# First keys of the attention as whole rows with turns behind them, retention's gated groups last, backward states beside the chunks

## The chip, the cores and the metric

One NeuronCore of a Trainium2 chip runs the whole program. The metric is the device time of one execution in microseconds; the median of the runs counts. TensorE is called PE below, its weight loads PEld, VectorE DVE, ScalarE ACT, GpSimd POOL, and SyncE, whose queue issues most DMAs, SP.

## The reference

Two layers of a hybrid block run over 1024 latent tokens (a grid of 16 rows by 64 columns) and 256 context tokens, with a model width of 1024, all in fp32.

```python
h = rms_norm(x, norm_w) * (1.0 + scale) + shift
(na_q, na_k, na_v, gla_q, gla_k, gla_v, gla_g, ret_q, ret_k, ret_v, z, g) = split_cols(h @ w_in)
na_l, na_c = na_branch(...)     # window of 8 x 16 neighbours and all context tokens, softmax
gla_l, gla_c = gla_branch(...)  # chunk scan in both directions, gated decay
ret_l, ret_c = ret_branch(...)  # chunk scan in both directions, fixed decay, rotated q and k
# merge_branches, i over (na, gla, ret):
y = y + sigmoid(gs[i]) * ((outs[i] * silu(zs[i])) @ w_branch[i])
x = x + gate * (y @ w_out)
```

A scan carries a state per head from chunk to chunk, forward and backward, and the context tokens come first in both directions. The second layer computes no context outputs. Queries and keys of retention are rotated for the latent tokens only.

## The kernel before, in words

Every large product is one of three products of a split into a high and a low float32r part (`mms`). One stream of such products, called the GEMM stream here, runs through the whole program: `projections` computes column groups of `w_in` in the order retention, GLA, attention v, attention q/k, the 12 g groups, the six z groups in the order of `Z_ORDER`, and `merge` goes on with `w_branch` and `w_out`. `fm` runs a group feature by feature in blocks of 512, 512 and 256 tokens (layer 1: 512 and 512), `tm` token by token.

The order of all instructions is made by `Drv.slot`, called a turn here. In a turn every worker (`drv.spawn`) and the GEMM stream advance twice, each GEMM advance by 3072 x `drv.mult` columns; then evacuations, and the lane (`attention_lane`) advances once; then the weight loader may issue a load (`load_raw`) or a conversion (`conv`: one ACT cast, two POOL subtractions). A `yield` in a lane costs a turn, in a worker half a turn. Where the GEMM stream only yields, PE gets the workers' matmuls alone.

The lane runs `retention`, `gla` and `na` one after the other, each as soon as its projections are done. The two scans have a first phase for all chunks of 128 tokens (c = 8 and 9 are context), which puts chunk states into `S` and passes on the forward ones; then a loop over c = 8 to 1 with `state_step` passes on the backward states, 4 DVE instructions for each c, two c's for each turn; then the second phase computes outputs, one worker for each chunk from 0 up: in `retention` rotation on DVE (`rope`), transposes on PE (`ret_t`), scores and outputs; in `gla` seven levels of decay on POOL, ACT and DVE, with products `gla_lv` on PE. `post` norms an output, transposes it (`post_t`) and stores it.

`na` works on four pairs of heads p, each with 8 window units and, in layer 0, 2 context units. `load_k(p)` loads the keys: two tiles `ks`, each with 64 rows of `nkh` twice, one above the other, and a tile `kl` of low parts. `pair` loads queries and bias, and three turns later issues the scores (`na_sw`, `na_sc`), then softmax, transposes (`na_ptw`, `na_ptc`) and the outputs (`na_o`). A new pair starts every three turns, and the next p's keys are loaded between them, one DMA a turn.

In `z_evac` the gate z is multiplied with a branch's output: groups 0 and 1 belong to the attention, 2 and 3 to GLA, 4 and 5 to retention. z0 and z1 wait until the attention's outputs are stored. For 0 to 3 the result goes to DRAM; for retention it becomes the high and low operand tiles `br`, with which `merge` begins.

Of the kernel before, what the change touches and what calls it, by code (L numbers as in the profile page):

```python
# [36 lines left out]
BR_ORDER = (2, 1, 0)  # L37
Z_ORDER = (2, 3, 0, 4, 5, 1)

# [69 lines left out]
def hybrid_kernel(ctx: ExitStack, tc: tile.TileContext, A: dict, out: bass.AP):  # L109
# [404 lines left out]
    def retention(layer):  # L514
        d = L[layer]
        with tc.tile_pool(name=f"ret{layer}", bufs=2) as pr, tc.tile_pool(name=f"retc{layer}", bufs=1) as prc:
# [59 lines left out]
            yield from lane_join(ws)  # L576
            for c in range(8, 0, -1):
                state_step(S, HI, c, _next_b(c), lambda h: RET_G[1][h])
                if c % 2:
                    yield  # L580
# [49 lines left out]
            drv.mult = RT_M  # L630
            ws = []
            for c in range(d["nt"]):
                ws.append(drv.spawn(phase2(c)))
                yield
# [4 lines left out]
    def gla(layer):  # L639
        d = L[layer]  # L640
        with tc.tile_pool(name=f"gla{layer}", bufs=2) as pl, tc.tile_pool(name=f"glac{layer}", bufs=1) as plc:
# [113 lines left out]
            yield from lane_join(ws)  # L755
            for c in range(8, 0, -1):
                state_step(S, HI, c, _next_b(c), lambda h: dec[HI, c, h:h + 1])
                if c % 2:
                    yield
# [107 lines left out]

            ws = []
            for c in range(d["nt"]):
                ws.append(drv.spawn(phase2(c)))  # L870
                for i in range(GL_N):
                    drv.mult = GL_M[2] if d["done"].get("nqk") else GL_M[1]
                    if i < 8 or not d["done"].get("nqk"):
                        yield
# [4 lines left out]
    def na(layer):  # L879
        d = L[layer]  # L880
        ntok, last = d["ntok"], d["last"]
        with tc.tile_pool(name=f"na{layer}", bufs=2) as pn:
# [7 lines left out]
            def load_k(p):  # L890
                ks = [pn.tile([P, NTOK], F32R, tag=f"k{hd}", name=f"k{hd}", bufs=2) for hd in range(2)]
                kl = pn.tile([P, NTOK], F32R, tag="kl", name="kl", bufs=2)
                tiles["k", p] = ks, kl
                for t0 in range(0, NTOK, 256):
                    ts = slice(t0, t0 + 256)
                    for hd in range(2):
                        r = p * P + 64 * hd
                        dma(fv(ks[hd][:, ts]), d["nkh"][r:r + 64, ts].unsqueeze(0).to_broadcast([2, 64, 256]))
                        yield
                    dma(fv(kl[:, ts]), d["nkl"][p * P:(p + 1) * P, ts])  # L900
                    yield
# [153 lines left out]
            def both(p):  # L1055
                yield from load_k(p)
                yield from load_v(p)

            for _ in both(0):
                pass  # L1060
            for _ in range(2):
                yield
# [44 lines left out]
    def projections(layer):  # L1107
# [34 lines left out]

        def fm(g, ns, evac):
            need(g)
            for m in range(g.w // P):
                for t0, nn in blocks(ns[m]):
                    yield from fm_unit(g, m, h, t0, nn, evac)
            g.done = True
# [91 lines left out]
        def z_evac(zi):  # L1240
            def f(m, t0, nn, ps):
# [8 lines left out]
                def w():  # L1250
                    yield
                    yield
                    if br == 2:
# [3 lines left out]
                        sc.copy(hi, st[:, :nn])  # L1257
                        gp.tensor_tensor(lo, st[:, :nn], fv(hi), op=ALU.subtract)
                    else:
                        gp.tensor_tensor(st[:, :nn], st[:, :nn], ot[:, :nn], op=ALU.mult)  # L1260
# [3 lines left out]

        per_pair = 2 if last else 3
        for zi in Z_ORDER:
            if zi < 2:
                while d.get("na_out", 0) < 2 * (zi + 1) * per_pair:
                    yield
            if zi == 0:  # L1270
                d["want_E"] = True
            if zi == 4:
                while not d.get("E"):
                    yield
            yield from fm(G["z"][zi], [ntok] * 2, z_evac(zi))
        d["done"]["z"] = True


    def merge(layer):
# [61 lines left out]
        for bi, br in enumerate(BR_ORDER[:2]):  # L1341
# [5 lines left out]
            for mg in range(4):  # L1347
                g = G["wb"][br][mg]
                need(g)
                for m in range(2):  # L1350
                    for t0, nn in blocks(ntok):
                        yield from unit(g, br, bi, 2 * mg + m, t0, nn)
                g.done = True
# [284 lines left out]
```

## Time and profile before

| what | us |
|---|---|
| median of 3 runs | 2954.19 |
| lowest, highest | 2953.34, 2956.12 |
| the profiled execution | 2957.61 |
| its span, first to last instruction | 2955.8 |
| PE busy in it | 2825.7 |

The profile is of one execution. A wait is the idle time of an engine before an instruction, put down to what came last. The granted clock is given as a share: 1.00 is 2.4 GHz and 0.50 is 1.2 GHz.

### The profile page before, as it was taken

How to read it: one execution, taken by the hardware profiler on the slowest of the kernel's cores; microseconds unless marked ns; L12 is line 12 of the kernel's file. 1: busy time of each engine (PE TensorE's matmuls, PEld its weight loads, DVE VectorE, ACT ScalarE, POOL GpSimd, SP SyncE). 2: the span in 40 equal slices, each digit the busy share in tenths (PEclk: the TensorE clock that was granted, in tenths of full speed). 3: DMA queues.
4: the chain of work that ended last, by engine and by line, in shares of the span. 5: the costliest groups of instructions: out<-in, count | busy, mean ns of one | idle time of the engine just before them, and what ended most of it. 6: DMA issues, size and time to landing. Idle time of an engine off the chain costs nothing.

```text
span 2955.8 us, 51865 instructions
## 1 busy us (share of the span) xinstructions
PE 2825.7 (96%) x19776; PEld 2434.3 (82%) x19776; DVE 1555.9 (53%) x3261; ACT 1065.8 (36%) x2443; POOL 1097.8 (37%) x1010
## 2 busy tenths in 40 slices
PE   7999999899979999799999999999999799989999
PEld 4999997678768888577899999997788688867889
DVE  5156468776715455523441536468977156662431
ACT  4123456533414433421121422456644144442210
POOL 4232126555611122042664432215766111214473
PEclk9999999999989999999999999999999899999999
DMA  6344443333235546458534444444443355555633
GB/s 238 107 137 125 140 119 111 108 118 113 85 119 149 160 147 184 123 159 270 162 109 140 124 152 125 130 136 118 138 120 108 124 165 166 180 157 159 210 125 108
DMA packets 394090, 418.69 MB, mean 142 GB/s; under 512 B 33949, under 2 KB 314285, under 8 KB 393841
## 3 DMA queue, kind: packets, MB, share of 16 engines
q1 hardware_dynamic: 356480, 361.59, 40.7%
q10 hardware_dynamic: 37360, 53.79, 5.2%
q8 instruction: 156, 2.56, 0.4%
q14 instruction: 94, 0.76, 0.1%
HBM read 302.72 MB, written 112.54 MB: 140 GB/s over the span
## 4 chain that ended last, share of the span: by engine, by line
PE 79%; DVE 6%; issue 5%; POOL 3%; DMA 3%; ACT 2%; SPq 2%; POOLq 0%; ACTq 0%; DVEq 0%
PE fm L376 34%; PE tm L376 19%; PE mg L376 10%; PE na_o L1028 3%; PE gla_lv L806 2%; SPq L116 2%; POOL wlo L345 1%; PE na_ptw L962 1%; DVE eq L836 1%; PE na_sw L919 1%; DMA k<-nkh 1%; PE na_ptc L964 1%; DVE eq L837 1%; PE na_sw L920 1%; PE gla_cum L711 1%
## 5 line engine op out<-in xcount | busy, mean ns | idle before, releaser
L376 PE MATMUL fm<-h,whi 128*128 128x512 f32 (+1 forms) x3936 | 920.9, 379 | 0.0
L345 POOL TENSOR_TENSOR wlo<-wraw,whi 128x512 fp32r<-128x512 f32 (+1 forms) x336 | 458.1, 1384 | 1006.5 <-ACT whi L342 817.9
L376 PEld LDWEIGHTS fm<-h,whi 128*128 128x128 f32 x3936 | 678.8, 190 | 149.9 <-issue 28.8
L376 PE MATMUL fm<-h,wlo 128*128 128x512 f32 (+1 forms) x1968 | 471.1, 375 | 0.0
L376 PEld LDWEIGHTS fm<-h,wlo 128*128 128x128 f32 x1968 | 340.3, 189 | 68.1 <-issue 5.9
L376 PE MATMUL tm<-whi,h 128*128 128x256 f32 (+1 forms) x2528 | 343.8, 285 | 5.5 <-DVE st_o L1376 2.4
L376 PEld LDWEIGHTS tm<-whi,h 128*128 128x128 f32 x2528 | 320.5, 190 | 7.4 <-ACT h L295 2.9
L342 ACT CAST whi<-wraw 128x1024 fp32r<-128x1024 f32 (+1 forms) x168 | 175.4, 1047 | 267.3 <-PE tm L376 128.3
L376 PE MATMUL tm<-wlo,h 128*128 128x256 f32 (+1 forms) x1264 | 188.0, 286 | 0.0
L376 PEld LDWEIGHTS tm<-wlo,h 128*128 128x128 f32 x1264 | 166.7, 190 | 0.7 <-issue 0.2
L835 DVE TENSOR_TENSOR ek<-dd,kd 128x512 f32<-128x512 f32 x108 | 107.3, 993 | 85.4 <-ACT dd L826 85.3
L376 PE MATMUL tm<-whi,yy 128*128 128x256 f32 x1152 | 147.8, 280 | 0.0
L791 POOL TENSOR_TENSOR dd<-Ac,ash 128x256 f32<-128x256 f32 x126 | 118.2, 938 | 69.4 <-DVE ash L778 53.1
L376 PEld LDWEIGHTS tm<-whi,yy 128*128 128x128 f32 x1152 | 140.7, 188 | 0.1
L836 DVE SCALAR_TENSOR_TENSOR eq<-dd,g_col,qd 128x256 f32<-128x256 f32 x126 | 121.4, 964 | 4.9 <-ACT dd L826 4.7
L826 ACT ACTIVATE dd<-dd 128x512 f32<-128x512 f32 x126 | 78.3, 628 | 124.8 <-POOL dd L792 122.6
L1248 DVE SCALAR_TENSOR_TENSOR st_z<-st_z,fm 128x512 f32<-128x512 f32 (+1 forms) x60 | 37.8, 633 | 156.5 <-ACT st_z L1247 153.7
L1232 ACT ACTIVATE st_g<-fm 128x512 f32<-128x512 f32 (+1 forms) x120 | 66.4, 553 | 149.1 <-PE fm L376 102.8
L792 POOL TENSOR_TENSOR dd<-ash,Ac 128x256 f32<-128x256 f32 x126 | 113.2, 899 | 0.0
L1376 DVE TENSOR_TENSOR st_o<-tm,gb 128x256 f32<-128x256 f32 x72 | 30.5, 424 | 155.2 <-PE tm L376 128.8
L416 DVE COPY st_tm<-tm 128x256 f32<-128x256 f32 (+1 forms) x59 | 25.3, 428 | 159.5 <-PE tm L376 154.0
L1320 DVE SCALAR_TENSOR_TENSOR gt<-gt,mg 128x512 f32<-128x512 f32 (+1 forms) x80 | 50.7, 633 | 108.0 <-PE mg L376 98.5
(1574 smaller groups left out, 4706.1 us busy)
## 6 DMA issues: line engine op xcount, KB each, us to landing
wraw<-in_w_in SPq DMA_DIRECT2D x104, 512.0 KB
wt<-in_w_mod SPq DMA_DIRECT2D x48, 512.0 KB
gd<-st_g ACTq DMA_DIRECT2D x96, 256.0 KB
gt<-gd SPq DMA_DIRECT2D x96, 256.0 KB
bt<-in_na_bm SPq DMA_DIRECT2D x32, 384.0 KB
ot<-o SPq DMA_DIRECT2D x48, 256.0 KB
wraw<-in_w_branch SPq DMA_DIRECT2D x24, 512.0 KB
k<-nkh SPq DMA_DIRECT2D x80, 128.0 KB
```

The lines of the kernel that those rows point to most:

```text
L116: nc.sync.dma_start(dst, src)
L342: sc.copy(hi[:, :, :w], raw[:, :, :w])
L345: gp.tensor_tensor(lo[:, ks, :w], raw[:, ks, :w], fv(hi[:, ks, :w]), op=ALU.subtract)
L376: pe.matmul(ps, a(k), b(k), start=i == 0, stop=i == tot - 1)
L791: gp.tensor_tensor(dv[:, :, Lh:], av[:, :, Lh:], rv, op=ALU.subtract)
L792: gp.tensor_tensor(dv[:, :, :Lh], rv, av[:, :, :Lh], op=ALU.subtract)
L806: pe.matmul(pl_[bk, x, h, :], ek_[:, h, bk], eq_[:, h, bk if lv else bq], start=True, stop=True)
L826: sc.activation(E_, E_, AF.Exp)
L835: ve.tensor_tensor(ek_, E_, kd_, op=ALU.mult)
L836: ve.scalar_tensor_tensor(eq[:, :, Lh:], ev[:, :, Lh:], rsc, qv[:, :, Lh:], op0=ALU.mult, op1=ALU.mult)
L1028: pe.matmul(po[64 * hd:64 * hd + 64, 0:P], ch[i][0], ch[i][1], start=i == 0, stop=i == n - 1)
L1232: sc.activation(st[:, :nn], ps, AF.Tanh, scale=0.5)
```

## The change

Five places change. In both scans the loop that passes on the backward states becomes a worker of its own (`back`), spawned together with the second phase; it steps one c for each half turn. The second phase takes the chunks from the last one down. In `na` the first pair's keys come as whole rows of 1280 tokens (3 DMAs in place of 15), the lane gives up one turn ahead of the first DMA and one behind each DMA, and four turns more, in place of two, ahead of the first pair. `Z_ORDER` moves group 1 ahead of 4 and 5. The last group, 5, runs block by block, and the units of the merge's first two branches wait until all four z units of their token block were issued.

```diff
-Z_ORDER = (2, 3, 0, 4, 5, 1)
+Z_ORDER = (2, 3, 0, 1, 4, 5)
...
                 ws.append(drv.spawn(phase1(c)))
                 yield
             yield from lane_join(ws)
-            for c in range(8, 0, -1):
-                state_step(S, HI, c, _next_b(c), lambda h: RET_G[1][h])
-                if c % 2:
+            def back():
+                for c in range(8, 0, -1):
+                    state_step(S, HI, c, _next_b(c), lambda h: RET_G[1][h])
                     yield
 
             def phase2(c):
@@ -628,8 +628,8 @@
             yield
             yield
             drv.mult = RT_M
-            ws = []
-            for c in range(d["nt"]):
+            ws = [drv.spawn(back())]
+            for c in reversed(range(d["nt"])):
                 ws.append(drv.spawn(phase2(c)))
                 yield
             yield from lane_join(ws)
...
                 yield
                 yield
             yield from lane_join(ws)
-            for c in range(8, 0, -1):
-                state_step(S, HI, c, _next_b(c), lambda h: dec[HI, c, h:h + 1])
-                if c % 2:
+            def back():
+                for c in range(8, 0, -1):
+                    state_step(S, HI, c, _next_b(c), lambda h: dec[HI, c, h:h + 1])
                     yield
 
             while not d["done"].get("glaq"):
@@ -865,8 +865,8 @@
                 yield
                 yield from post(pl, po, gain, d["o"][1], c, att.rearrange("p h t -> p (h t)"), (5, 2))
 
-            ws = []
-            for c in range(d["nt"]):
+            ws = [drv.spawn(back())]
+            for c in reversed(range(d["nt"])):
                 ws.append(drv.spawn(phase2(c)))
                 for i in range(GL_N):
                     drv.mult = GL_M[2] if d["done"].get("nqk") else GL_M[1]
@@ -891,11 +891,12 @@
                 ks = [pn.tile([P, NTOK], F32R, tag=f"k{hd}", name=f"k{hd}", bufs=2) for hd in range(2)]
                 kl = pn.tile([P, NTOK], F32R, tag="kl", name="kl", bufs=2)
                 tiles["k", p] = ks, kl
-                for t0 in range(0, NTOK, 256):
-                    ts = slice(t0, t0 + 256)
+                piece = 256 if p else NTOK
+                for t0 in range(0, NTOK, piece):
+                    ts = slice(t0, t0 + piece)
                     for hd in range(2):
                         r = p * P + 64 * hd
-                        dma(fv(ks[hd][:, ts]), d["nkh"][r:r + 64, ts].unsqueeze(0).to_broadcast([2, 64, 256]))
+                        dma(fv(ks[hd][:, ts]), d["nkh"][r:r + 64, ts].unsqueeze(0).to_broadcast([2, 64, piece]))
                         yield
                     dma(fv(kl[:, ts]), d["nkl"][p * P:(p + 1) * P, ts])
                     yield
@@ -1056,9 +1057,10 @@
                 yield from load_k(p)
                 yield from load_v(p)
 
+            yield
             for _ in both(0):
-                pass
-            for _ in range(2):
+                yield
+            for _ in range(4):
                 yield
             drv.mult = NA_M1
             for p in range(4):
@@ -1140,11 +1142,13 @@
                     ga.done = True
             gb.done = True
 
-        def fm(g, ns, evac):
+        def fm(g, ns, evac, by_block=False):
             need(g)
-            for m in range(g.w // P):
-                for t0, nn in blocks(ns[m]):
-                    yield from fm_unit(g, m, h, t0, nn, evac)
+            units = [(m, t0, nn) for m in range(g.w // P) for t0, nn in blocks(ns[m])]
+            if by_block:
+                units.sort(key=lambda u: u[1])
+            for m, t0, nn in units:
+                yield from fm_unit(g, m, h, t0, nn, evac)
             g.done = True
 
         yield from tm2(G["ret"][0], G["ret"][1], NT, spill_tm(d["ret"], 256, 256), spill_tm(d["ret"], 512, 256))
...
                         hi, lo = bt.get(0, ro // P, t0, nn), bt.get(1, ro // P, t0, nn)
                         sc.copy(hi, st[:, :nn])
                         gp.tensor_tensor(lo, st[:, :nn], fv(hi), op=ALU.subtract)
+                        d["z_out"][t0] = d["z_out"].get(t0, 0) + 1
                     else:
                         gp.tensor_tensor(st[:, :nn], st[:, :nn], ot[:, :nn], op=ALU.mult)
                         drv.defer(lambda: dma(d["b"][br][ro:ro + P, t0:t0 + nn], st[:, :nn]))
@@ -1263,6 +1268,7 @@
             return f
 
         per_pair = 2 if last else 3
+        d["z_out"] = {}
         for zi in Z_ORDER:
             if zi < 2:
                 while d.get("na_out", 0) < 2 * (zi + 1) * per_pair:
@@ -1272,7 +1278,7 @@
             if zi == 4:
                 while not d.get("E"):
                     yield
-            yield from fm(G["z"][zi], [ntok] * 2, z_evac(zi))
+            yield from fm(G["z"][zi], [ntok] * 2, z_evac(zi), zi == 5)
         d["done"]["z"] = True
 
 
@@ -1349,6 +1355,8 @@
                 need(g)
                 for m in range(2):
                     for t0, nn in blocks(ntok):
+                        while d["z_out"].get(t0, 0) < 4:
+                            yield
                         yield from unit(g, br, bi, 2 * mg + m, t0, nn)
                 g.done = True
         while not w1["done"]:
```

On SP, at the start of the attention in layer 0, eight rows in a row before (the last of five equal rounds of keys, then the first pair's loads; `k` are the two tiles `ks`, `wraw` weights, `bt` bias):

```order
L116 DMA k_9010<-nkh_106 128x1x256
L116 DMA k_9011<-nkh_106 128x1x256
L116 DMA kl<-nkl_107 128x256
L116 DMA vcx<-nv_104 128x2x128
L116 DMA wraw_9061<-in_w_in 128x4x256
L116 DMA q<-nq_105 128x2x128
L116 DMA qz_9006<-nq_105 64x128 x2
L116 DMA bt<-in_na_be 128x2x288
```

and now, from the last store of GLA's outputs on:

```order
L116 DMA o_0_94<-att 128x4x128
L116 DMA wraw_8934<-in_w_in 128x4x256
L116 DMA k_8951<-nkh_106 128x1x1280
L116 DMA k_8952<-nkh_106 128x1x1280
L116 DMA kl<-nkl_107 128x1280
L116 DMA vcx<-nv_104 128x2x128
L116 DMA wraw_9048<-in_w_in 128x4x256
L116 DMA q<-nq_105 128x2x128
L116 DMA qz_8930<-nq_105 64x128 x2
L116 DMA bt<-in_na_be 128x2x288
```

Three key DMAs stand where 15 stood, with the same 128 partitions and five times the columns, and a weight load stands between the store and the first key. On PE, 91,648 columns of GEMM matmuls stand between GLA's last transposes and the first score in layer 0, in place of 48,640; in layer 1 92,160 in place of 49,152.

On DVE, at the start of the merge in layer 1, before (`fm` are z units, here of group 1; `mg` merge units, `y` the merge's sum, `bg` the GLA operands):

```order
L1248 SCALAR_TENSOR_TENSOR st_z_28081<-st_z_28081,fm_28032 128x512
L1255 TENSOR_TENSOR st_z_28081<-st_z_28081,ot_28079 128x512
L1248 SCALAR_TENSOR_TENSOR st_z_28123<-st_z_28123,fm_28066 128x512
L1248 SCALAR_TENSOR_TENSOR st_z_28154<-st_z_28154,fm_28108 128x512
L1248 SCALAR_TENSOR_TENSOR st_z_28193<-st_z_28193,fm_28139 128x512
L1248 SCALAR_TENSOR_TENSOR st_z_28237<-st_z_28237,fm_28178 128x512
L1318 SCALAR_TENSOR_TENSOR y10_0_28210<-gt_28218,mg_28220 128x512
```

and now, where the z units are of group 5 and `ot` is retention's output:

```order
L1252 SCALAR_TENSOR_TENSOR st_z_28128<-st_z_28128,fm_28080 128x512
L1259 TENSOR_TENSOR st_z_28128<-st_z_28128,ot_28126 128x512
L1252 SCALAR_TENSOR_TENSOR st_z_28168<-st_z_28168,fm_28113 128x512
L1259 TENSOR_TENSOR st_z_28168<-st_z_28168,ot_28166 128x512
L1252 SCALAR_TENSOR_TENSOR st_z_28213<-st_z_28213,fm_28153 128x512
L1324 SCALAR_TENSOR_TENSOR y10_0_28186<-gt_28194,mg_28196 128x512
L1259 TENSOR_TENSOR st_z_28213<-st_z_28213,ot_28211 128x512
```

The multiplication of the last z unit with `ot`, from which `br` is made, now stands behind the evacuation of the merge's first unit.

## Rows read from the trace of the kernel before

**Rows 1.** The page: span, busy time by engine, granted clock in 40 slices.
```profile
span 2955.8 us, 51865 instructions
...
PE 2825.7 (96%) x19776; PEld 2434.3 (82%) x19776; DVE 1555.9 (53%) x3261; ACT 1065.8 (36%) x2443; POOL 1097.8 (37%) x1010
...
PEclk9999999999989999999999999999999899999999
```

**Rows 2.** The waits of PE: instruction, releaser, us in total, times, longest.
```profile
PE na_sw L919 <- DMA bt<-in_na_be: 34.7, 2, 17.8
PE na_o L1028 <- DVE PT L983: 23.2, 16, 1.7
...
PE gla_lv L806 <- DVE eq L837: 16.7, 9, 5.3
...
PE ret_t L597 <- DVE qk L541: 2.8, 2, 2.5
```

**Rows 3.** Time line, PE, attention start: start us, duration, instruction, count, idle before.
```profile
837.66 0.60 PE L488 MATMUL post_t<-ident,att 128*128 128x128 f32 x4
...
878.17 0.58 PE L919 MATMUL na_sw<-k,q 128*128 128x288 f32 x1 [17.80 <-DMA bt<-in_na_be]
...
2316.60 0.60 PE L488 MATMUL post_t<-ident,att 128*128 128x128 f32 x4
...
2356.36 0.58 PE L919 MATMUL na_sw<-k,q 128*128 128x288 f32 x1 [16.91 <-DMA bt<-in_na_be]
```

**Rows 4.** Time line of SP's queue, first keys of layer 0 and of layer 1.
```profile
841.83 1.12 SPq L116 DMA_DIRECT2D k<-nkh  x2
...
866.36 3.21 SPq L116 DMA_DIRECT2D kl<-nkl  x1
...
2320.56 1.10 SPq L116 DMA_DIRECT2D k<-nkh  x2
```

**Rows 5.** Stretches: window, length, busy us of PE, PEld, DVE, ACT, POOL, clock, DMA.
```profile
846.00:850.00 4.00, 4.00 (x19) 3.24 (x18) 0.00 (x0) 1.53 (x2) 0.78 (x1) 1.00 0.14 48
...
878.20:882.60 4.40, 4.40 (x14) 3.91 (x15) 2.20 (x10) 1.16 (x5) 0.00 (x0) 0.50 1.01 293
2356.40:2360.60 4.20, 4.20 (x14) 3.68 (x15) 1.97 (x8) 1.08 (x4) 0.00 (x0) 0.50 0.98 300
```

**Rows 6.** Stretches, same columns: the ends of the attention in layers 0 and 1.
```profile
1183.00:1242.60 59.60, 42.02 (x336) 34.56 (x336) 42.44 (x138) 28.22 (x99) 7.18 (x6) 0.90 0.36 106
2597.00:2655.00 58.00, 43.48 (x361) 36.17 (x359) 43.73 (x139) 28.85 (x100) 6.68 (x6) 0.91 0.47 140
```

**Rows 7.** Retention in layer 0: a time line row, a stretch, all state steps (min/median/max ns).
```profile
220.34 1.02 PE L597 MATMUL ret_t<-ident,qk 128*128 128x128 f32 x4 [2.53 <-DVE qk L541]
...
220.30:223.80 3.50, 3.46 (x16) 3.49 (x17) 2.36 (x6) 0.59 (x1) 0.00 (x0) 0.52 0.38 115
...
L503 DVE SCALAR_TENSOR_TENSOR S<-S x128: 273/290/1455, 157.4 to 1782.6; 64x128 f32<-64x128 f32 x128
```

**Rows 8.** GLA's second phase: three stretches, and PE's waits from 600 to 830 us.
```profile
450.00:600.00 150.00, 136.13 (x919) 108.58 (x918) 126.05 (x196) 81.92 (x160) 86.03 (x80) 0.97 0.41 120
...
2030.00:2140.00 110.00, 104.24 (x693) 82.75 (x692) 102.33 (x153) 66.25 (x128) 73.02 (x67) 0.98 0.44 123
2140.00:2310.00 170.00, 170.00 (x1320) 136.64 (x1319) 124.83 (x171) 70.85 (x158) 108.87 (x108) 1.00 0.41 119
...
PE gla_lv L806 <- DVE eq L837: 7.2, 3, 2.4
```

**Rows 9.** z groups of layer 1, groups (busy us, mean ns, idle); then the merge's start.
```profile
L1258 POOL TENSOR_TENSOR br<-st_z,br 128x512 fp32r<-128x512 f32 x8 | 10.3, 1290 | 71.0 <-ACT br L1257 71.0
L1248 DVE SCALAR_TENSOR_TENSOR st_z<-st_z,fm 128x512 f32<-128x512 f32 x12 | 8.2, 687 | 53.7 <-ACT st_z L1247 53.7
...
L1255 DVE TENSOR_TENSOR st_z<-st_z,ot 128x512 f32<-128x512 f32 x8 | 6.9, 861 | 4.5 <-DMA ot<-o 4.3
...
L1257 ACT CAST br<-st_z 128x512 fp32r<-128x512 f32 x8 | 5.0, 621 | 17.0 <-DVE st_z L1255 17.0
...
2727.92 2.02 PE L376 MATMUL mg<-br,whi 128*128 128x512 f32 x8
...
2730.71 2.02 PE L376 MATMUL mg<-br,whi 128*128 128x512 f32 x8
```

## The prediction

> **What bounds the kernel now.** I read the page first: PE is busy for 2825.7 us of the 2955.8 us span, so all that can be won without taking work away is about 130 us of idle PE, and what the lower clock costs behind it [rows 1]. The list of waits of PE says who ends that idle time [rows 2]. The largest entry is the first score of the neighbourhood attention (`na_sw`), 34.7 us in only two waits, one per layer; behind it stand the outputs `na_o` at the end of that attention, then `gla_lv`. The time lines then show what is in the two large waits [rows 3, 4]. In layer 0 the last transposes of the GLA stage end at 838.26; PE then has GEMM work until 860.37 and stands still until 878.17 (17.80 us). SP issues the first keys at 841.83 and is still issuing key pieces at 869.57. So the load chain, from the first key to the first score, takes 36.3 us, and the work put over it 22.1 us. Layer 1 has the same picture: transposes end 2317.20, keys 2320.56, PE is out of work at 2339.45, score at 2356.36, so 35.8 us against 22.3 us. Last, the table by stretches: when PE comes back, the granted clock is 0.50, the lower level of 1.2 GHz, for 4.4 and 4.2 us [rows 5].
>
> **The start of the attention: room behind the first load.** The program order gives what the added turns put there: between the last GLA transposes and the first score stood 48,640 columns of GEMM matmuls in layer 0 and stand 91,648 now; in layer 1 49,152 and 92,160. The price of a column is read from this very stretch: 22.11 us / 48,640 = 0.4546 ns, and 22.25 / 49,152 = 0.4527 ns [rows 3]. So the cover grows to 41.7 us in both layers. Of that 3.6 and 3.4 us pass before SP can issue the first key (it waits for the last store of the GLA outputs, as before), which leaves 38.1 and 38.4 us against chains of 36.3 and 35.8. The wait goes, with 2 us to spare, even if whole rows are no faster than pieces.
>
> Are they faster? While the key pieces move, the DMA share is 0.14, which is about two of the 16 engines, at 48 GB/s [rows 5]. The slow DMAs are the two per piece that read 64 rows twice. 1.31 MB at 48 GB/s is 27 us, about the whole issue time of 28 us. The new DMAs have the same outer shape (twice 64 rows) with longer rows, so I take the chain as unchanged. It can't be shorter than about 15 us: 1.97 MB of keys at the 293 GB/s of [rows 5] is 7 us, and 8.6 us follow the last key. It can be longer by the weight loads that now stand in this stretch of SP's queue, one more in layer 0 and two in layer 1 (512 KB at 293 GB/s, 1.8 us each): 38.1 us against 38.1, and 39.4 against 38.4, a stall of 1 us. I take 0, and keep 0 to 5 us per layer.
>
> The Trainium skill (DMA: Bandwidth & Descriptors, section "Why a DMA increments its semaphore by 16 and not by 1") says that such a DMA runs on the largest number of engines, at most 16, that divides the slowest dimension of both sides; for twice 64 rows that is two. The trace's share of 0.14 agrees. The rule speaks against the first half of this part: longer rows leave the load where it was, and all of the gain comes from the room; the sum is the same by it.
>
> What goes: 17.80 + 16.91 = 34.7 us of idle PE, and of the 4.4 and 4.2 us that PE ran busy at half speed one half, 4.3 us. Together **-39.0 us**.
>
> **The end of the attention.** The GEMM work put ahead of the attention is missing at its end. There the z groups wait for the attention's outputs, and PE runs attention pairs alone. Counted in the driver's turns (calls of `slot`), the GEMM stream emits nothing in the last 32 turns of layer 0 and 30 of layer 1; with the change it is 37 and 37. The stretches cost this today [rows 6]: layer 0 has 59.6 - 42.0 = 17.6 us idle, and at a mean clock of 0.90 some 12 us are at the lower level, of which PE is busy 0.7, which costs 4.2 us; 21.8 us over 32 turns is 0.68 a turn. Layer 1: 14.5 idle and 3.9 for the clock, 0.61 a turn. Five and seven more turns: 3.4 + 4.3 = **+7.7 us**.
>
> **Backward states beside the chunks, chunks from the last one down.** The lane loses the turns in which it only stepped states, so retention's and GLA's second phases start some four turns earlier against the GEMM work. PE's work is the same, so this alone is worth nothing; what counts are the single waits. In layer 0, retention's first transposes waited 2.53 us for the rotation of chunk 0, and the 3.5 us after it ran at 0.52 of the clock [rows 7]. Now the first two chunks are context, which is not rotated: that wait goes, 2.53 + 1.7 = **-4.2 us** (at worst the wait returns for a later chunk, 0). In layer 1 chunk 7 is rotated, and state steps of 4 x 0.290 us [rows 7], two per turn, stand among its DVE work; 2.3 us per turn is about the size of a wait like the one in layer 0. I take +0.5, from 0 to +4.
>
> GLA's second phase is the part that I can't settle. Its waits come where a weight conversion or a norm of the attention's keys falls into the same turn as a chunk's level. In layer 0 the three chunks beside the q/k projections cost 150 - 136.1 = 13.9 us idle and 4 us for the clock; in layer 1, the same code in another phase, 5.8 and 2 us; then the rest of layer 0 has three waits of 2.4 us, and the rest of layer 1 not one in 170 us [rows 8]. The change shifts both phases. For layer 0 I take the middle between its 18 us and layer 1's 8, **-5 us** (-10 to +5). From the order, the conversions of its seven later chunks come at the same offsets as now, in another succession, and three of them again hit the bad one: 0. For layer 1 I take **+1.5 us**, between 0 and +10, the price of layer 0.
>
> **z groups.** Today z1 (attention) runs between the last retention group z5 and the merge. Now z5 is last and the merge begins with its result. In layer 1 the merge's second unit needs the last unit of z5. The order on DVE shows the chain: after the end of z5 its tanh and product, then the result of the merge's first unit, which ends 2.8 us later (2727.92 to 2730.71) and takes 0.69, then the multiplication with the outputs 0.86, ACT's cast 0.62, POOL's subtraction 1.29 [rows 9]. The high half is there 2.8 + 0.69 + 0.86 + 0.62 = 5.0 us after the end of z5; PE wants it after 2.8. That is 2.2 us of wait, a little more for the low half, and 1.7 us if the clock falls as it did in [rows 7]: **+3.5 us** (2 to 5). In layer 0 two 256-column units lie between, and the same chain just fits: +0.5. That z1 runs earlier is worth nothing: no wait of PE on its results is in the list [rows 2], and the GEMM work still waits for the end of the attention at the same place.
>
> **The sum.** -39.0 + 7.7 - 4.2 + 0.5 - 5 + 1.5 + 3.5 + 0.5 = -34.5 us. The profiled execution took 2957.6 us (its span 2955.8), so 2923.1; the median of the three runs is 2954.2, 3.4 us below the profiled one, so **2920 us**.
>
> **The rivals.** (a) The key load isn't covered: 38 us stand against 36, and SP's queue gets weight loads between keys and pair. If whole rows or the extra loads make the chain 45 us, each layer stalls 7 us and loses 2 to the clock: +18, 2938 us. For it: the margin is thin. Against it: the chains of the two layers agree within 0.5 us. (b) GLA falls badly: layer 1 gets layer 0's waits (+10) and layer 0 wins nothing (+5): with -5 and +1.5 undone, 2938. For it: the stall count depends on coincidences; against it: layer 1's earliest two chunks keep their offsets. (c) The gain comes back at the end of the attention: all 43,008 columns put ahead (19.5 us per layer) return as idle time there instead of 3.4 and 4.3. Then -39.0 + 39, and the rest leaves about 2951. For it: PE is in deficit there today; against it: the count of turns. (d) Slower: a whole-row DMA runs on one engine instead of two. Its 1.31 MB then take 55 us, the chain 63, and a stall of 25 us per layer stands where 17.4 stood: +15 on the starts and +4.5 from the other terms, 2974. It decides from a chain of about 53 us on. For it: a shape that no row shows. Against it: the outer dimension is unchanged.
>
> **How the numbers follow.** Forecast 0.72; (a) 0.10, (b) 0.10, (c) 0.04, (d) 0.04. Forecast alone: 2910 to 2930. To hold 8 in 10 the range also takes in (a) and (b) and the better ends of the GLA term: 2908 to 2938. A measurement of this kernel can tell about 0.2%, 5.9 us, from no change: faster 0.92 (forecast, a, b), same 0.04 (c), slower 0.04 (d).
>
> **What would show it.** The waits of PE: `na_sw` on `bt` gone or under 5 us in total; `na_o` on `PT` up from 23 to some 29 us; `ret_t` on `qk` gone in layer 0; a new wait of 2 to 3 us of `mg` on `br` at layer 1's merge. The time line of SP: the two whole-row keys still some 13 us each. The GLA windows tell the term I couldn't settle. The forecast is wrong if the first score waits for keys, if the stretch without GEMM work is much over 37 turns long in time (over 75 us), or if `gla_lv` waits grow by more than 10 us.

## The result, and the profile after

The changed kernel is slower: a median of 2982.4 us against 2954.9 us, a ratio of 1.0090 with a 95% interval of 1.0077 to 1.0103. The prediction was 2920 us (2908 to 2938), faster. The profiled execution has a span of 2980.8 us, 25.0 more than [rows 1], and splits almost evenly: PE is busy 12.4 us longer and idle 12.6 us longer. The page, then the waits of PE (instruction, releaser, us in total, times, longest):

```profile
span 2980.8 us, 51811 instructions
...
PE 2838.1 (95%) x19776; PEld 2436.4 (82%) x19776; DVE 1548.3 (52%) x3261; ACT 1064.0 (36%) x2443; POOL 1089.3 (37%) x1010
```

```profile
PE na_o L1029 <- DVE PT L984: 35.4, 19, 10.2
PE mod_ps L210 <- DMA wt<-in_w_mod: 20.7, 17, 6.5
PE gla_lv L806 <- DVE eq L837: 17.6, 11, 3.5
PE na_ms L1185 <- ACT nsq L1179: 14.9, 9, 4.3
PE post_t L488 <- DVE att L483: 9.9, 8, 1.4
PE na_o L1029 <- ACT PT L987: 9.4, 6, 3.1
PE fm L376 <- ACT st_g L1236: 8.2, 2, 4.9
PE nrm_t L284 <- DVE nt L270: 4.9, 6, 1.9
PE gla_lv L806 <- DVE eq L836: 4.7, 4, 2.9
PE mg L376 <- ACT br L1261: 2.1, 1, 2.1
```

The 34.7 us of `na_sw` [rows 2] are gone, as forecast. In their place stand many smaller entries, and `fm` waiting for ACT, which was not there before.

PE's matmuls are the same in all the kernels below. So there are points in the program where two kernels have run exactly the same GEMM columns and the same other matmuls. The table says by how much each stage took longer than in the kernel before (us, from start times on PE at such points in the two profiled executions; minus is a gain).

| stage | predicted | after | keys alone | scans alone | z alone |
|---|---|---|---|---|---|
| retention, layer 0 | -4.2 | -3.9 | 0 | -4.2 | 0.1 |
| GLA, layer 0 | -5 | +8.0 | -0.1 | +7.9 | 0.3 |
| attention, layer 0 | -16.6 | -8.6 | -0.7 | -7.6 | +3.7 |
| merge, layer 0 | +0.5 | -3.2 | -3.2 | -0.9 | +0.8 |
| start and retention, layer 1 | +0.5 | +2.1 | +1.3 | +0.2 | 0 |
| GLA, layer 1 | +1.5 | **+22.1** | -1.2 | **+20.6** | -1.5 |
| attention, layer 1 | -14.7 | **+4.6** | -2.6 | -3.0 | **+5.5** |
| merge, layer 1 | +3.5 | +3.9 | 0 | 0 | +3.9 |
| sum | -34.5 | +25.0 | -6.5 | +13.0 | +12.8 |

The predicted attention is the first-key term and the end-of-attention term together, by layer. The three right-hand columns are the first three experiments.

### The profile page after: what moved, and what is told of

The parts are those of the page before. It is cut to its first block, busy times and chain, and to the rows that moved or that the text cites. A ratio compares the mean times of both kernels' runs of the same rounds, so it can differ in the third digit from the quotient of the medians.

```text
span 2980.8 us, 51811 instructions
## 1 busy us (share of the span) xinstructions
PE 2838.1 (95%) x19776; PEld 2436.4 (82%) x19776; DVE 1548.3 (52%) x3261; ACT 1064.0 (36%) x2443; POOL 1089.3 (37%) x1010
## 4 chain that ended last, share of the span: by engine, by line
PE 46%; DVE 6%; issue 3%; DMA 2%; ACT 1%; POOL 1%; SPq 0%; ACTq 0%; POOLq 0%; DVEq 0%
PE fm L376 17%; PE tm L376 10%; PE mg L376 10%; PE na_o L1029 2%; DMA wraw<-in_w_in 1%; DVE eq L837 1%; DVE eq L836 1%; POOL st_o L1385 1%; PE gla_lv L806 1%; PE mod_ps L210 1%; PE na_sw L920 1%; DVE Sg L503 1%; DVE nst L938 1%; DVE ek L835 1%; POOL wlo L345 1%
## 5 line engine op out<-in xcount | busy, mean ns | idle before, releaser
L1265 POOL TENSOR_TENSOR st_z<-st_z,ot 128x512 f32<-128x512 f32 (+1 forms) x40 | 48.1, 1207 | 252.7 <-DMA ot<-o 101.8
L836 DVE SCALAR_TENSOR_TENSOR eq<-dd,g_col,qd 128x256 f32<-128x256 f32 x126 | 110.6, 878 | 10.8 <-ACT dd L826 10.8
L837 DVE SCALAR_TENSOR_TENSOR eq<-dd,g_col,qd 128x256 f32<-128x256 f32 x126 | 109.2, 867 | 0.0
```

The costliest lines, as they stand in the source:

```text
L836: ve.scalar_tensor_tensor(eq[:, :, Lh:], ev[:, :, Lh:], rsc, qv[:, :, Lh:], op0=ALU.mult, op1=ALU.mult)
L837: ve.scalar_tensor_tensor(eq[:, :, :Lh], ev[:, :, :Lh], lsc, qv[:, :, :Lh], op0=ALU.mult, op1=ALU.mult)
```

## The experiments

### The parts one by one

e1_keys takes over the `load_k` and turn edits alone, e2_scans the `back` workers and reversed chunks alone, e3_z `Z_ORDER`, `by_block` and `z_out` alone. e4_gla_old is the changed kernel with GLA as before, its state loop ahead of the second phase again:

```diff
-            ws = [drv.spawn(back())]
-            for c in reversed(range(d["nt"])):
+            ws = []
+            for c in range(d["nt"]):
```

> The kernel before with the first keys as whole rows and the added turns alone; scans and z groups as before. Theory A (the loss of the change sits in GLA, where the new order of the scan sets other coincidences; the attention still gains): by the two traces at equal work the attention of layer 0 gained 8.6 us and that of layer 1 lost 4.6, 10 of it in one wait of na_o at its end, which should not come back without the other parts: 2938 to 2951 us. Theory B (the room's gain comes back at the end of the attention, which is longer by 5 and 7 turns without GEMM work): 2955 to 2972 us.

> The kernel before with the backward states beside the chunks and the chunks from the last one down, in both scans, alone. Theory A: retention -4, GLA of layer 0 +8, of layer 1 +22, so 2974 to 2986 us, and gla_lv, na_ms and post_t wait some 20 us more in all. Theory B: the scans are worth nothing or little, 2948 to 2958 us.

> The kernel before with the new order of the z groups, its last group by blocks and the wait of the merge, alone. Both theories: +3.5 us for the first wait of mg on br in layer 1 and -3 to +1 in layer 0, 2953 to 2960 us.

> The kernel after with GLA as before (states passed on ahead, chunks from 0 up); retention, first keys and z groups as after. Theory A: the 30 us of GLA go, 2945 to 2957 us. Theory B: the time stays, 2975 to 2985 us.

Measured, as ratios to the kernel before: keys alone 0.9977 (0.9967 to 0.9986; 2948.5 us), scans alone 1.0055 (1.0042 to 1.0068; 2973.2 us), z alone 1.0045 (1.0033 to 1.0058; 2970.4 us), GLA undone 1.0017 (1.0008 to 1.0026; 2960.8 us). The parts nearly add up: -2.3 + 5.5 + 4.5 = 7.7 thousandths against 9.0. GLA is the largest loss, as theory A said, though two runs lie just outside the ranges of that theory (2973.2 us against 2974 to 2986, 2960.8 against 2945 to 2957). With GLA as before the changed kernel is 21.6 us faster, less than the 30 us that its two GLA stages lose: the attention of layer 0 then takes 3.0 us longer than before, where it took 8.6 less, and the scans alone lose 7.9 us in that layer's GLA and gain 7.6 in its attention. Why the attention gains what GLA loses there is not shown. Both theories missed on z, and the keys gained only 7 us where the prediction had 31 (-39.0 + 7.7). So three things needed a cause.

### Why the keys gain so little: the slow load holds ACT

In the run with the keys alone PE stands still in layer 0 once more, only elsewhere. PE, then ACT's time line (start us, duration, instruction, count, idle before and its end; ACTq rows are stores issued by ACT), then SP's queue:

```profile
878.73 5.65 PE L376 MATMUL fm<-h,whi 128*128 128x512 f32 x16 [8.94 <-ACT st_g L1234]
```

```profile
855.88 0.38 ACT L1234 ACTIVATE st_g<-fm 128x256 f32<-128x256 f32 x1 [2.23 <-PE fm L376]
877.15 0.83 ACTq L119 DMA_DIRECT2D gd<-st_g  x2
878.08 0.60 ACT L1234 ACTIVATE st_g<-fm 128x512 f32<-128x512 f32 x1 [21.81 <-DMA bt<-in_na_be]
```

```profile
841.73 1.12 SPq L116 DMA_DIRECT2D k<-nkh  x2
844.24 11.37 SPq L116 DMA_DIRECT2D wraw<-in_w_in  x1
855.65 6.69 SPq L116 DMA_DIRECT2D kl<-nkl  x1
```

ACT issues the stores of the g groups itself. In this program the DMAs of SP and ACT take eight semaphores in turn, and in its instruction stream the store at 877.15 waits on the semaphore that `kl` (855.65) took before it. `kl` stands in the queue behind the slow key rows. ACT does nothing for 21.81 us, the GEMM's PSUM tiles, into which PE writes its products, are not emptied, and PE stops for 8.94 us. (The releaser printed, `bt`, is only what came last.) The changed kernel has the same in both layers: PE stops for 3.26 us in layer 0 and for 4.95 us in layer 1. Layer 0, PE and then ACT:

```profile
868.85 6.50 PE L376 MATMUL fm<-h,whi 128*128 128x512 f32 x16 [3.26 <-ACT st_g L1236]
```

```profile
867.77 0.38 ACTq L119 DMA_DIRECT2D gd<-st_g  x1
868.20 0.87 ACT L1236 ACTIVATE st_g<-fm 128x512 f32<-128x512 f32 x2 [14.99 <-DMA vcx<-nv]
```

If the slow load is the root, making it fast must do what the room was meant to do. k64 is the kernel before with no added turn and, for the first pair only, this edit (the low parts `kl` as whole rows too; the rest of the loop is left out here):

```diff
-    dma(fv(ks[hd][:, ts]), d["nkh"][r:r + 64, ts].unsqueeze(0).to_broadcast([2, 64, 256]))
+    dma(fv(ks[hd][0:64, ts]), d["nkh"][r:r + 64, ts])
+    dma(fv(ks[hd][64:P, ts]), d["nkh"][r:r + 64, ts])
```

e1_k64 adds the change's turns to it, so it differs from the keys alone only in the key DMAs (four of 64 rows in place of two of twice 64). room_pieces has the change's turns and the old 15 pieces.

> The kernel before, and only the first pair's keys in another shape: whole rows, and each half of a key tile by a DMA of its own with 64 rows (5 DMAs in place of 15); no added turns. Theory S (the first load is slow because its DMAs run on two engines; with 64 rows they run on all): the first key to the first score takes some 15 us in place of 36, less than the 22 us of work above it: both waits of 17 us go, nothing is taken from the end of the attention, 2912 to 2926 us. Theory T (the chain is long for other reasons, the queue of SP and the loads behind the keys): 10 us of each wait stay, 2936 to 2952 us.

> The whole rows with the added turns, and the keys by DMAs of 64 rows. Theory S: the wait of ACT's stores for the slow keys goes (8.9 us of PE in layer 0), the longer end of the attention stays: 2928 to 2942 us, and slower than the same keys without added turns. Theory T: as with the added turns alone, 2945 to 2952 us.

> The added turns of the change with the keys in 15 pieces as before (five pieces, then a turn); nothing else changed. If the whole rows matter by their length (one row holds a store of ACT behind it for the whole of its time), layer 0 loses its 8.9 us of waiting for ACT's g blocks: 2936 to 2944 us. If any keys on two engines do it, in pieces or in rows, 2944 to 2953 us, as with whole rows.

k64: 0.9873 (0.9859 to 0.9886), 2918.6 us. e1_k64: 0.9936 (0.9923 to 0.9948), 2937.5 us. room_pieces: 0.9967 (0.9956 to 0.9979), 2947.4 us, and `fm` waits 8.77 us for ACT at the same place as with whole rows; so the length of the rows does not matter. Theory S holds. In e1_k64 `fm` no longer waits for ACT, and against the keys alone it gains 4.1 thousandths, some 12 us. In k64 the keys come fast; a stretch of it (window, length, busy us of PE, PEld, DVE, ACT, POOL, clock, DMA share, GB/s), then SP and PE at layer 0's start:

```profile
845.00:851.00 6.00, 6.00 (x27) 4.86 (x27) 0.00 (x0) 1.53 (x2) 1.60 (x3) 1.00 1.04 288
```

```profile
842.26 2.50 SPq L116 DMA_DIRECT2D k<-nkh  x4
...
854.79 0.38 SPq L116 DMA_DIRECT2D bt<-in_na_be  x1
```

```profile
860.63 0.30 PE L925 MATMUL na_sw<-k,q 128*128 128x288 f32 x1
```

The DMA share is 1.04 and 288 GB/s where it was 0.14 and 48 [rows 5]. From the first key to the first score it takes 18.4 us in place of 36.3, and this lies under GEMM work that was there all along: no idle time is left before the score. The Trainium skill (DMA: Bandwidth & Descriptors, section "Rules for kernel authors") asks for an outermost dimension that is a multiple of 16 if a DMA is to use all engines; the share of 1.04 agrees.

### What the room costs at the end of the attention

e1_k64 and k64 differ in the added turns alone, and the turns cost 18.9 us. The program order has 41 and 39 turns without GEMM work at the ends of the attention in e1_k64, 32 and 30 in k64. Those stretches, e1_k64 first, then k64 (columns as above):

```profile
1154.40:1229.60 75.20, 53.72 (x418) 44.16 (x418) 48.63 (x170) 35.19 (x122) 7.05 (x6) 0.84 0.38 114
2558.10:2634.40 76.30, 56.24 (x449) 46.66 (x447) 55.65 (x179) 36.62 (x126) 7.63 (x6) 0.89 0.46 136
```

```profile
1163.30:1221.00 57.70, 39.85 (x336) 32.61 (x336) 42.52 (x138) 28.27 (x99) 7.18 (x6) 0.94 0.37 110
2558.70:2615.40 56.70, 42.51 (x365) 35.05 (x363) 43.75 (x139) 29.09 (x100) 6.45 (x5) 0.94 0.48 143
```

Idle time grows from 17.9 + 14.2 to 21.5 + 20.1, 9.5 us for 18 turns or 0.53 a turn, which is what [rows 6] said. The rest agrees with an estimate for the clock. In layer 0 a mean of 0.84 over 75.2 us is 24 us at the lower level; 0.94 over 57.7 us is 7. With PE busy for some 70% of that time and half of it lost, the two layers together lose some 10 us more than in k64. The prediction had priced the clock at 0.13 us a turn; by this estimate it cost about 0.5. So the forecast for the keys, -31.3 us, failed in two terms of like size: some 12 us for ACT's stores, and some 11 for the turns (18.9 us in place of 7.7).

In the changed kernel the same two ends, and the longest wait of PE in the second, with ACT's rows ahead of it:

```profile
1173.00:1236.50 63.50, 43.66 (x361) 35.68 (x358) 44.22 (x150) 32.86 (x113) 7.08 (x6) 0.95 0.42 124
2593.30:2671.90 78.60, 52.89 (x440) 43.79 (x438) 52.14 (x175) 36.51 (x126) 6.54 (x5) 0.89 0.46 134
```

```profile
2604.52 1.79 PE L1029 MATMUL na_o<-PT,vw 96*64 96x128 f32 x11 [10.16 <-DVE PT L984]
```

```profile
2602.23 0.33 ACTq L119 DMA_DIRECT2D o<-oN  x1
2602.68 0.60 ACT L1251 ACTIVATE st_z<-fm 128x512 f32<-128x512 f32 x1 [6.12 <-DMA ot<-o]
```

Their idle time is 45.6 us where it was 32.1 [rows 6]. The store at 2602.23 waits, in the instruction stream, on the semaphore of a store of SP (`b`): the coupling of the start once more.

Is it the turns without GEMM work as such? NA_M1 sets the columns per turn during the attention, and a smaller one spreads the same columns over more turns. e1_k64_m64 is e1_k64 with `NA_M1 = 0.64`; k64_ret is k64 with retention as after; k64_ret_m6 and k64_ret_m5 set NA_M1 to 0.6 and 0.5 in it.

> The keys by DMAs of 64 rows, without added turns, and retention's second phase as after (states beside the chunks, from the last one down). Retention of layer 0 gave 4 us in three runs: 2911 to 2917 us against 2918.6 for the keys alone. If the shifted phase of GLA costs as much: 2916 to 2924 us.

> Whole rows in DMAs of 64 rows, the added turns, and 0.64 for NA_M1 in place of 0.7, which spreads the same GEMM columns over more turns of the attention: by the program order 23 and 25 turns without GEMM work at its end in place of 41 and 39. If the loss of the added turns is the turns without GEMM work: the 19 us come back, 2910 to 2922 us. If the room costs elsewhere, or thinner turns stall: 2932 to 2942 us.

> Keys by DMAs of 64 rows, no added turns, retention as after, NA_M1 0.6: 11 and 15 turns without GEMM work in place of some 31 and 30. If such turns cost what the end of the attention showed (some 1 us each), 35 of them are 20 to 35 us: 2880 to 2896 us. If thinner turns stall in the middle of the attention as much: 2908 to 2918 us.

> As the last, with NA_M1 0.5: 3072 columns a turn and no turn without GEMM work at the end of the attention. By the first theory 2872 to 2888 us; if 3072 columns (1.39 us) no longer cover a turn of the attention, waits of na_o on PT come back all over it: 2890 to 2910 us.

k64_ret: 0.9856 (0.9839 to 0.9872), 2914.4 us; retention's gain of 4 us is real. But thinner work gave nothing: 2939.6 us (0.9951, 0.9936 to 0.9966), 2920.0 us (0.9882, 0.9865 to 0.9899) and 2923.8 us (0.9892, 0.9878 to 0.9907). The theory fell in this form, and the two runs without added turns came out above both ranges given for them. The idle time had moved into the middle of the attention, where `na_o` now waited for ACT: in k64_ret_m6 15.4 us in 10 waits. In e1_k64_m64 the longest, 4.92 us at 1117.04, stands behind a store of ACT that waits, in the instruction stream, on the semaphore of a later pair's key piece: the same coupling. So the last three runs gave all pairs whole rows by DMAs of 64 rows (cut to the lines that matter):

```diff
-                piece = 256 if p else NTOK
+                piece = NTOK
...
+                        dma(fv(ks[hd][0:64, ts]), d["nkh"][r:r + 64, ts])
+                        dma(fv(ks[hd][64:P, ts]), d["nkh"][r:r + 64, ts])
```

kall_ret is k64_ret with that, kall_ret_m6 has NA_M1 0.6, kall_ret_room the change's turns.

> The keys of all four pairs as whole rows by DMAs of 64 rows, no added turns, retention as after. In the middle of the attention hardly a wait was left with the first pair's keys alone, so 2908 to 2916 us (2914.4 with the first pair's keys alone); no theory expects more than a few us here.

> As the last, with NA_M1 0.6 (11 and 15 turns without GEMM work). If the slow later keys held ACT's stores: na_o's waits on PT from ACT fall under 1 us each, and the time to 2888 to 2904 us. If what is lost is the GEMM columns that cover the attention, wherever the gap lies: 2912 to 2922 us.

> As the first, with the added turns of the change. If the slow later keys are what made the added turns cost 19 us: 2910 to 2922 us. If it is the GEMM columns taken from the attention: 2926 to 2938 us, 15 to 22 us over the same kernel without them.

kall_ret: 0.9854 (0.9840 to 0.9869), 2912.3 us. kall_ret_m6: 0.9796 (0.9781 to 0.9811), 2896.1 us, the fastest of all, 2% under the kernel before. kall_ret_room: 0.9926 (0.9909 to 0.9942), 2934.3 us, 22 us over kall_ret: the slow later keys are not what makes the added turns dear. PE's waits on ACT, k64_ret_m6 first, then kall_ret_m6:

```profile
PE na_o L1034 <- ACT PT L992: 15.4, 10, 3.3
```

```profile
PE na_o L1030 <- ACT PT L988: 3.1, 3, 2.0
```

The longest is still 2.0 us, not under 1 as expected, but the total falls to a fifth.
Thinner work does pay here, 16.2 us for the 35 turns without GEMM work that it removes (0.46 a turn), where it cost 2.6 thousandths, some 8 us, with the slow later keys. That the slow loads ahead of ACT's stores make this difference is what the waits above suggest; the later keys changed in shape and in number of DMAs at once, and no run separates the two.

### Why GLA loses 22 us in layer 1

The change does two things to GLA in layer 1, besides turning the chunks round. It takes four turns out ahead of the second phase, and it steps the states beside the first chunk. Once the q/k projections of layer 1 are done, a chunk takes eight turns and a weight conversion comes every four, so the offset of conversions to chunks stays the same to the end: 3, 7, 11, 15 turns behind a chunk's start before, 1, 5, 9, 13 after. g_shift drops only the four turns; g_new_y4 has GLA as after with four turns given back; g_rev only reverses the chunks.

```diff
 g_shift:   state_step(S, HI, c, _next_b(c), lambda h: dec[HI, c, h:h + 1])
-           if c % 2:
-               yield
 g_new_y4:
+           for _ in range(4):
+               yield
            ws = [drv.spawn(back())]
 g_rev:
-           for c in range(d["nt"]):
+           for c in reversed(range(d["nt"])):
```

> The kernel before, and only the four turns gone in which GLA's lane steps the backward states; states stepped ahead of the second phase, chunks from 0 up, as before. By the program order this sets the weight conversions of layer 1 to turns 1, 5, 9, 13 after the start of each of its last chunks, where they stand at 3, 7, 11, 15. Theory P (the loss in GLA comes from this offset): 2964 to 2976 us, post_t waits 1.4 us once per chunk in layer 1. Theory R (it comes from the reversed chunks or from state steps among their work on DVE): 2946 to 2957 us, as before.

> The kernel before with GLA as after (states beside the chunks, chunks from the last one down), and four turns given up ahead of the second phase, so that all offsets are those of before. Theory P: 2950 to 2960 us, no waits of post_t and gla_lv over those of before in layer 1. Theory R: 2966 to 2980 us.

> The kernel before, and only GLA's chunks from the last one down; the states are stepped ahead of them, in four turns, as before. If the steps beside the first chunk cost the 9 us that stood in layer 1 with all offsets as before, the time is that of before, 2950 to 2960 us, and gla_lv has no wait over 1 us in 2025 to 2070 us. If the reversed order costs them: 2962 to 2974 us.

g_shift: 1.0035 (1.0021 to 1.0048), 2968.2 us, with GLA of layer 1 13.5 us later by the same points as in the table. g_new_y4: 1.0056 (1.0042 to 1.0070), 2973.1 us, GLA of layer 1 +9.1. g_rev: 0.9995 (0.9985 to 1.0004), 2955.7 us. Neither theory alone was right: the four turns give 13.5, the state steps 9.1, together 22.6 of 22.1, and the order of the chunks nothing. Layer 0's GLA comes apart in the same way: by the same points g_shift is 5.4 us later there and g_new_y4 2.9, together 8.3 of 8.0. (The median of g_new_y4 is 3 us above what the two profiles show, which I did not follow.)

How the offset costs: DVE, then POOL and PE in the changed kernel, one of five like places in layer 1 (five waits of 1.37 us, 6.9 of the 13.5):

```profile
2171.55 0.48 DVE L836 SCALAR_TENSOR_TENSOR eq<-dd,g_col,qd 128x256 f32<-128x256 f32 x1
...
2173.96 1.51 DVE L836 SCALAR_TENSOR_TENSOR eq<-dd,g_col,qd 128x256 f32<-128x256 f32 x1
2175.40 1.51 DVE L837 SCALAR_TENSOR_TENSOR eq<-dd,g_col,qd 128x256 f32<-128x256 f32 x1
2176.83 1.32 DVE L483 TENSOR_TENSOR att<-att,pss 128x512 f32<-128x512 f32 x1
```

```profile
2173.45 3.17 POOL L345 TENSOR_TENSOR wlo<-wraw,whi 128x512 fp32r<-128x512 f32 x2
```

```profile
2178.30 0.63 PE L488 MATMUL post_t<-ident,att 128*128 128x128 f32 x4 [1.37 <-DVE att L483]
```

While POOL converts a weight, the same DVE operation takes 1.51 us instead of 0.48. The Trainium skill (SBUF — State Buffer, section "SBUF: two separate sides") says that a DVE operation with two SBUF inputs and a POOL operation that reads SBUF lock each other out of a port they share; the 1.51 against 0.48 us agree.

In the offset of after, the product that `post_t` needs (`att`, 2176.83) stands right behind it, once for each chunk. In the kernel before that product began ahead of the conversion and took 0.68 us, DVE and then POOL:

```profile
2172.53 0.68 DVE L483 TENSOR_TENSOR att<-att,pss 128x512 f32<-128x512 f32 x1
```

```profile
2172.71 3.36 POOL L345 TENSOR_TENSOR wlo<-wraw,whi 128x512 fp32r<-128x512 f32 x2 [0.38 <-issue]
```

Of the rest of the 13.5 us, 3.6 are one wait of `gla_lv` in g_shift; in the changed kernel it is 3.5 us long, and norms of the attention's q/k stand on DVE ahead of the level. What is left is not taken apart.

How the state steps cost: DVE and PE in g_new_y4, where all offsets are those of before:

```profile
2035.08 0.48 DVE L837 SCALAR_TENSOR_TENSOR eq<-dd,g_col,qd 128x256 f32<-128x256 f32 x1
2035.60 3.11 DVE L503 SCALAR_TENSOR_TENSOR Sg<-Sg,dec 64x128 f32<-64x128 f32 x8
2038.74 0.69 DVE L835 TENSOR_TENSOR ek<-dd,kd 128x512 f32<-128x512 f32 x1
```

```profile
2039.88 1.41 PE L806 MATMUL gla_lv<-eq,ek 128*64 128x64 f32 x15 [3.57 <-DVE eq L836]
```

Two steps a turn, 3.11 us, stand ahead of the first chunk's level, whose product then waits 3.57 us. With the steps ahead of the chunks (g_rev) that wait is gone.

### Why the new order of the z groups loses 9 us beside the merge

z_alt changes `Z_ORDER` alone in e3_z, to (2, 3, 0, 4, 1, 5).

> The z groups as after, but group 4 ahead of group 1 (2, 3, 0, 4, 1, 5; 5 by blocks and the wait of the merge stay). Theory Z (of the 13 us of the z part, 9 come from the end of the attention, where z1 starts later than z4 did and the weights wt are then waited for by mod_ps; the rest from the merge): 2955 to 2962 us, mod_ps waits for wt gone, the wait of mg on br still there. Theory Y (the loss is in the merge and its waits): 2966 to 2972 us.

z_alt: 1.0005 (0.9996 to 1.0015), 2958.1 us; theory Z holds. In the stages above the +3.7 and +5.5 us of the attentions become about 0, and the +3.9 of layer 1's merge stay. (By the traces z_alt takes back 8.7 us of e3_z, by the medians 12.3; the difference is not explained.) PE behind the last outputs of layer 1, in e3_z and then in z_alt:

```profile
2659.62 1.67 PE L376 MATMUL fm<-h,whi 128*128 128x512 f32 x6
2664.07 0.86 PE L210 MATMUL mod_ps<-wt,csi 128*2 128x256 f32 x8 [2.78 <-DMA wt<-in_w_mod]
```

```profile
2654.83 3.97 PE L376 MATMUL fm<-h,whi 128*128 128x512 f32 x16
2658.64 0.62 PE L376 MATMUL fm<-h,wlo 128*128 128x512 f32 x2
2659.39 0.61 PE L210 MATMUL mod_ps<-wt,csi 128*2 128x256 f32 x8
```

When the attention's tiles are freed, the weights `wt` of the next modulation are loaded and soon used. z4 waits for the same event as that load, so 18 of its matmuls stand on PE before the first `mod_ps`. z1 waits for the stored outputs, and only 6 stand there: the load is no longer covered. PE waits for it 2.36 us in layer 0 and 2.78 in layer 1, and the mean granted clock of the 10 us from 2659.60 in e3_z is 0.83 (in the kernel before it is 1.00 over the 10 us from 2655.00); the waits alone are 5.1 of the 9.2 us.

## Why the prediction was wrong, step by step

- **What bounds the kernel, and the first waits.** Right: the waits were the loads, and the score no longer waits. k64 gives 38.9 us back, what [rows 3, 5] had promised as 39.0. Wrong was the step "the wait goes, with 2 us to spare". It counted what stands in SP's queue behind the keys, and not that ACT's stores take the same semaphores. By the traces the starts gave 26.5 us in place of 39.0: the idle time up to the first score fell from 17.8 to 3.3 and from 16.9 to 5.0 us, and what is left of it is `fm` waiting for ACT. The 4.3 us of the clock did not come: over the 9.8 us behind each of the new waits the granted clock is 0.72 and 0.85.
- **Whole rows no faster.** [Rows 5] were read rightly: a share of two engines, so rows bring nothing, and room_pieces bears it out (2947.4 against 2948.5 us). What I left unread in them was that the load itself could be mended.
- **The end of the attention.** Right mechanism, mis-sized term: +7.7 forecast, some +13 in the changed kernel, all of it idle time. Of this 10.16 us are the one wait in layer 1 shown above; no other kernel here shows one of that size. Without it the two ends would have grown by some 3 us in the changed kernel; what a turn costs is shown by e1_k64 against k64. With fast first keys the turns cost 1.05 us each, not 0.61 to 0.68, because the clock is at the lower level for longer, and there are 18 of them, not 12, when GLA isn't moved as well. Rival (c), the whole gain coming back there, had 0.04; in e1_k64 half of k64's gain does.
- **Retention.** Right: -3.9 us, and `ret_t` waits 0.6 us in all in place of 2.8 [rows 2].
- **GLA.** The step that failed most: -5 and +1.5 forecast, +8.0 and +22.1 measured in its stages. I called it the part I couldn't settle and took its middle. The price of a bad offset was taken from layer 0, where chunk and conversion periods differ and the bad offset comes and goes; in layer 1 it is locked and repeats with every chunk. The state steps on DVE were priced for retention's layer 1 (0.5 us) and not for GLA, where DVE is the engine PE waits for. Rival (b) had the sign, with half the size. In layer 0 the four turns (5.4) and the state steps (2.9) explain the +8.0, but which single waits the four turns set there is not taken apart.
- **z groups.** The merge was right: 2.08 us of wait, 3.9 in all, and 0.8 in layer 0. Wrong was "that z1 runs earlier is worth nothing": the work that stands at the end of the attention covered the load of `wt`, and this cost about 9 us.
- **The range.** Chance 0.04 for slower rested on one exotic mechanism. It was not that one, but three ordinary terms (ACT's stores, GLA, z) that each fell to their bad side.

## What to carry to other kernels

Before making room for a slow load, ask why it is slow: another shape of the same transfer gave 39 us, the room 7. In this kernel a store issued by ACT made ACT wait for the transfer that held its semaphore, so a slow load must be looked for in the time lines of the compute engines that issue DMAs too. Where two periodic streams meet on one engine, compare their periods: where one is a multiple of the other, as in layer 1 here, the offset is locked and its wait repeats to the end of the loop, and taking a few turns out ahead of the loop changes it.

## What the runs showed of the hardware that I had not expected

- The same DVE operation took 0.48 us at one place and 1.51 us while POOL converted a weight.
- Twice 64 rows in one DMA ran at a DMA share of 0.14 and 48 GB/s; the same bytes as separate DMAs of 64 rows ran with all transfers at 1.04 and 288 GB/s.
- ACT stood still for 21.81 us because a store that it issues waited on the semaphore of a load issued by SP.
- At the end of the attention nine more turns without GEMM work took the mean granted clock from 0.94 to 0.84 in one layer and to 0.89 in the other; by the estimate above that cost as much as the added idle time itself.
